# A hybrid trunk step: first transfers chained, x tiles loaded ahead, mLSTM outputs turned one step later, first attention tiles in other memory

## The chip, the cores and the metric

The kernel runs on one core of a Trainium2 chip, as one launch. The metric is the device time of that core in microseconds (us), from the first to the last instruction with what the launch adds around them. In the profile PE is TensorE (PEld its weight loads), DVE is VectorE, ACT is ScalarE, POOL is GpSimd and SP is SyncE, which here only issues transfers.

## The reference

One inference step of a one-layer trunk: 2048 prompt tokens (one sequence) and 64 sample tokens (8 sequences of 8 tokens, each with 8192 past positions in a paged cache). Two groups of heads share one input projection and one output projection: 8 heads of forgetting attention (FoX, width 64) and 4 heads of mLSTM (width 128). Everything is float32.

```
z = x @ w_in                       # x: 2048 or 64 tokens x 1024; w_in: 1024 x 3600
fq, fk, fv, f-gate = z[...]        # FoX queries, keys, values, log forget gates
mq, mk = silu(conv4(z[qk part]))   # causal convolution over 4 tokens, per channel
mv, i-gate, f-gate, o-gate = z[...]
fox = softmax(fq fk^T / 8 + L_q - L_k) fv      # L: running sum of the log forget gates
C, n, m, h = mLSTM scan over chunks of (mq, mk, mv, gates)
mix = [fox, layernorm_per_head(h) * norm_w * sigmoid(o-gate)] @ w_o
x1 = layernorm(alpha x + mix)
y  = layernorm(alpha x1 + relu(x1 @ w1)^2 @ w2)
```

The sample tokens run the same with keys, values and forget gates gathered from the paged cache through `page_table`, and with the mLSTM and convolution states that are given. Outputs are y, the new k and v, the log forget gates and the new states.

## The kernel before

**Phases.** Phase A (0 to about 965 us) makes the input projection for four blocks of four prompt tiles of 128 tokens (the first block also has tile 16, the 64 sample tokens), and beside it the mLSTM and the first part of the sample attention. Phase B is the prompt's FoX attention, phase O the output projection, phase C the MLP, with the rest of the sample attention beside it. A matmul of full precision is three matmuls of split operands: `mm3` (lines 154 to 156) multiplies the high parts (`whi`, `xh`) and the two mixed products (`wlo`, `xl`). `split_hi` (line 146, ACT) and `split_lo` (line 149, DVE) make these parts.

**Order.** The Python code names the work in a program order; a scheduler then orders the instructions on each engine by that and by their dependences. `tick(us)` is called after each piece of matmul work with its length. It advances two side programs written as generators: `macc` (the gate streams and the mLSTM, a step for each 2.3 us) and `acc` (the sample attention, a step for each 5.6 us in phase A). `acc[0]` is the time on its clock, `acc[1]` the generator, `attend` makes one step of it.

**x.** `load_x` (line 263) loads a tile of x into `xn` (two buffers), turns it with eight transposes (`px`, line 278, in the ring `pm` of four PSUM tiles that the projection uses too) and splits it to `xh` and `xl`. In `natural` (line 415, tokens on the output's partitions) a hook loads and turns tile n + 2 ahead of tile n's matmuls. The first two tiles of the next block are loaded and turned by the last `natural` of a block and after the block. `wload` (line 228) loads a weight block as two pieces of 512 KB (`wra`, line 236) and splits them. All these transfers are issued by SP, in its order.

**The convolution** of block 0 (`qi`, `qs`, `ac`, `scT`, lines 456 to 498) is mostly DVE's work. Beside it starts `sample_attention`: its prologue makes the gather indices (`idxK`, `idxV`, lines 1289 and 1295) and running sums of the forget gates (`ri`, line 1321) on DVE. After four such steps it waits until `kx["new"]` is set, late in the first block.

**The mLSTM** (`m_block`, line 617) runs in 16 chunks of 128 tokens: scores `pS` (line 642), transposed keys `pk` (line 655), numerators `mn` (lines 665, 666), state (line 674), then `norm_out` (line 569), whose last steps are a multiplication on POOL (`hh`, line 582). The result is turned by four transposes on PE (line 587), copied by ACT (`ot`, line 589) and stored; `turn_out` does this in the next chunk, right after its scores. `pS`, the turned output, `pk` and `mn` share a ring `mm` of two PSUM tiles:

```
            V.scalar_tensor_tensor(Wm, pS, KSC, Wm, op0=OP.mult, op1=OP.mult)
            yield 1
            turn_out()
            while bi not in gated:
                yield 1
            og = pm.tile([128, 512], F32, name="og", bufs=1)
            SY.dma_start(og, dog[t0:t0 + 128])
            yield 1
            pk = ppm.tile([128, 4, 128], F32, name="mm", tag="mm", bufs=2)
```

**Phase B** goes through 64 units of a head and 256 queries. For the first, `head` makes the tiles `nl`, `vn`, `ks`, `ls`, `keys` loads (`dup`), doubles and turns keys, `queries` loads and splits queries (`qn`, `qh`). The pool of these tiles takes memory that phase A's tiles had, so a first writer can have to wait for their last reader.

Of the kernel before, what the change touches and what calls it, by code (L numbers as in the profile page):

```python
# [10 lines left out]
F32 = mybir.dt.float32  # L11
# [13 lines left out]
D = 1024  # L25
# [17 lines left out]
C_V = 2568  # L43
# [9 lines left out]
def body(ctx, tc, I, O, stages):  # L53
# [142 lines left out]
    def conv_setup():  # L196
# [19 lines left out]
        SY.dma_start(gbias[:, 12:16], dap(I["b_fg"], 0, [[0, 128], [1, 4]]))  # L216

    hist = pa.tile([128, 8, 3], F32, name="hist")
    V.memset(hist, 0.0)
# [6 lines left out]
    mend = pa.tile([4, 1], F32, name="mend")  # L226

    def wload(cols):

        n = sum(c[1] for c in cols)  # L230
        H, L = [], []
        for kg in range(2):
            wr = pa.tile([128, 4 * 272], F32, name="wra", bufs=2)[:, :4 * n].rearrange("p (k c) -> p k c", k=4)
            o = 0
            for c0, m in cols:
                SY.dma_start(wr[:, :, o:o + m], w_in[kg * 512:(kg + 1) * 512, c0:c0 + m].rearrange("(k p) c -> p k c", p=128))
# [25 lines left out]

    def load_x(bi, tiles):

        blk, pre, off = geom(bi)
        for t in tiles:
            i = int(off[t] >= pre + 256)
            if len(xT.setdefault(bi, [])) == i:
                w = 256 if i else 320
                xT[bi].append((pa.tile([128, 8, w], F32R, name=f"xh{i}"), pa.tile([128, 8, w], F32R, name=f"xl{i}")))  # L270
            n = tok_n(t)
            xn = pa.tile([128, D], F32, name="xn", bufs=2)
            SY.dma_start(xn[:n], x_of(t))
            (xh, xl), s = xcol(bi, t)
            for hf in range(2):
                px = ppa.tile([128, 4, 128], F32, name="px", tag="pm", bufs=4)
                for k in range(4):
                    T.transpose(px[:, k, :n], xn[:n, (hf * 4 + k) * 128:(hf * 4 + k + 1) * 128], ident[:n, :n])
                dh = xh[:, hf * 4:hf * 4 + 4, s]
                split_hi(dh, px[:, :, :n])  # L280
                split_lo(xl[:, hf * 4:hf * 4 + 4, s], px[:, :, :n], dh)

# [128 lines left out]
    def block_a(bi):  # L411
        blk, pre, off = geom(bi)
        t0 = blk[-4] * 128
        c0 = blk[-4]
        def natural(sink, *cols, hook=None):
            wh, wl = first.pop() if first else wload(cols)
            for i, t in enumerate(blk):
                if hook:
                    hook(i)
                m = tok_n(t)  # L420
                ps = ppa.tile([128, 512], F32, name="pm", tag="pm", bufs=4)[:m, :wh[0].shape[1]]
                (xh, xl), s = xcol(bi, t)
                for k in range(8):
                    mm3(ps, xh[:, k, s], xl[:, k, s], wh[k], wl[k], k == 0, k == 7)
                sink(t, m, ps)
                tick(2.6)

        def stage(ps, m, n):
            st = pa.tile([128, 256], F32, name="st", bufs=4)[:m, :n]
            A.copy(st, ps)  # L430
            return st

        for i in range(2):
            def sink(t, m, ps, i=i):
                r = tok_r(t)
                SY.dma_start(dv[r:r + m, i * 256:(i + 1) * 256], stage(ps[:, :256], m, 256))
                if i == 1:
                    V.tensor_copy((gats if t == 16 else gat[:, t])[:, 0:16], ps[:, 256:272])
            natural(sink, (C_V + i * 256, 256), *([(C_FF, 8), (C_I, 8)] if i == 1 else []),
                    hook=None if i else lambda n: load_x(bi, blk[n + 2:n + 3]))  # L440
        if bi == 0:
# [113 lines left out]
        for i in range(2):  # L555
            def sink(t, m, ps, i=i):
                d = v_out(t)[:, i * 256:(i + 1) * 256]
                SY.dma_start(d, stage(ps, m, 256))
            natural(sink, (1024 + i * 256, 256),
                    hook=None if i == 0 or bi == 3 else lambda n: load_x(bi + 1, BLKS[bi + 1][0:1]) if n == len(blk) - 1 else None)  # L560

# [55 lines left out]
    def m_block(bi):  # L617
# [10 lines left out]
        for c in range(bi * 4, bi * 4 + 4):  # L628
# [17 lines left out]
            yield 1  # L646
            turn_out()
            while bi not in gated:
                yield 1
            og = pm.tile([128, 512], F32, name="og", bufs=1)  # L650
            SY.dma_start(og, dog[t0:t0 + 128])
            yield 1
            pk = ppm.tile([128, 4, 128], F32, name="mm", tag="mm", bufs=2)
            for h in range(4):
# [168 lines left out]
    if "S" in stages:  # L823
        gen = sample_attention(tc, I, O, ps_, pps, cst, ident, sqk, dnl, dR, dmix, dqb, vx, kx, pa)
    load_x(0, [16])
    first = [wload([(C_V, 256)])]
    load_x(0, [0])
    for bi in range(4):
        g = block_a(bi)
        next(g)  # L830
        if bi == 0 and gen:
            acc[0], acc[1] = 0.0, gen
        macc[1].append(m_block(bi))
# [5 lines left out]
        if bi < 3:  # L839
            load_x(bi + 1, BLKS[bi + 1][1:2])  # L840
    while macc[1]:
# [8 lines left out]
    def phase_b():  # L850
# [14 lines left out]

        def head(h):
            nl = pb.tile([128, 2048], F32, name="nl", bufs=2)
            vn = pb.tile([128, 16, 64], F32, name="vn", bufs=2)
            ks = pb.tile([128, 2048], F32R, name="ks", bufs=2)
            ls = pb.tile([128, 32], F32, name="ls", bufs=2)  # L870
            G.memset(ls, 1.0)
            return dict(h=h, ls=ls, nl=nl, vn=vn, ks=ks)
# [13 lines left out]

        def keys(z, g):

            h = z["h"]
            kn = twice(kp[g * 512:(g + 1) * 512, h * 64:h * 64 + 64], 4)  # L890
            if h == 0 and g == 0:
                queries(z, 0)
            if h == 0:
# [99 lines left out]
        def finish(z, half):  # L993
# [9 lines left out]
            for q in range(2):  # L1003
# [4 lines left out]
                SY.dma_start(dmix[h // 2, (h % 2) * 64:(h % 2) * 64 + 64, o + q * 512:o + q * 512 + 512], ot[:, s])  # L1008

        units = [(h, g) for h in range(8) for g in range(8)]  # L1010
        Z = {0: head(0)}
        dmask = pb.tile([128, 128], F32, name="dmask")
        V.memset(dmask, 0.0)
        G.affine_select(dmask, dmask, pattern=[[-1, 128]], compare_op=OP.is_ge, fill=NEG, base=0, channel_multiplier=1)
        keys(Z[0], 0)
# [33 lines left out]
    acc[1] = acc[3]  # L1049
    if acc[1] is not None:  # L1050
        attend()

# [210 lines left out]
def sample_attention(tc, I, O, ps_, pps, cst, ident, sqk, dnl, dR, dmix, dqb, vx, kx, pa):  # L1263
# [309 lines left out]
    def step(n):  # L1573
# [84 lines left out]
```

## Time and profile before

| | |
|---|---|
| time, median of 3 runs | 3442.84 us (3429.21 to 3446.31) |
| the profiled execution | 3431.24 us, span 3429.5 us |
| mean granted TensorE clock | 0.983 |
| busy: PE, DVE, ACT, POOL | 96%, 63%, 40%, 26% |
| moved by DMA | 646.37 MB, mean 188 GB/s |

Rows of a timeline read: start, length, engine, line, operation, out<-in, shape, number of instructions drawn together, and in brackets the idle time of the engine ahead of it and what ended that. Rows of groups read: line, engine, operation, out<-in, shapes, number | busy us, mean ns | idle time before. Rows of windows: from:to, length, busy time of PE, PEld, DVE, ACT, POOL (with the number of instructions), granted clock (1.00 is full speed), share of the DMA engines, GB/s.

### The profile page before, as it was taken

The page shows a single profiled execution, that of the slowest core. Times are in us where ns is not written, and L with a number is a line of the kernel's source. Part 1 is how long each engine was busy: PE and PEld are TensorE (multiplying, and loading weights), DVE is VectorE, ACT ScalarE, POOL GpSimd, SP SyncE. Part 2 cuts the span into 40 slices and gives each one's busy share as a digit, 9 for nine tenths or more (in the row PEclk, how much of TensorE's full clock was granted, in tenths as well). Part 3 has the DMA queues.
Part 4 walks back from the last instruction along what each step waited for, and adds up shares of the span by engine and source line. Part 5 has one row for each costly group of instructions (what it writes and reads, how often), then busy time and mean ns, then how long its engine had stood idle before and what let it go on. Part 6 is the DMA issues. An engine that isn't in the chain of part 4 may idle for free.

```text
span 3429.5 us, 59557 instructions
## 1 busy us (share of the span) xinstructions
PE 3277.8 (96%) x22428; PEld 2675.2 (78%) x22428; DVE 2166.7 (63%) x5282; ACT 1367.5 (40%) x2818; POOL 892.0 (26%) x958
## 2 busy tenths in 40 slices
PE   8999989988979999999899999999999999999998
PEld 8999988888866666677577777777777777888887
DVE  5847657557558787655566666666666545655545
ACT  3332334333348888512323233332333333443332
POOL 0021222322332222276323324323324210100000
PEclk9999999999989999999899999999999999999999
DMA  5565764876753232487777777768668554442221
GB/s 170 133 204 160 226 203 141 293 227 202 237 178 89 75 82 58 139 284 250 257 248 255 246 236 260 273 227 301 231 209 305 199 185 151 154 139 81 82 85 65
DMA packets 427095, 646.37 MB, mean 188 GB/s; under 512 B 84092, under 2 KB 320960, under 8 KB 425912
## 3 DMA queue, kind: packets, MB, share of 16 engines
q1 hardware_dynamic: 350120, 363.35, 35.0%
q0 software_dynamic: 74304, 270.57, 21.5%
q10 hardware_dynamic: 2384, 8.65, 0.7%
q8 instruction: 177, 2.90, 0.3%
q14 instruction: 110, 0.90, 0.1%
HBM read 589.63 MB, written 52.83 MB: 187 GB/s over the span
## 4 chain that ended last, share of the span: by engine, by line
PE 43%; DMA 4%; issue 2%; DVE 1%; POOL 0%; ACT 0%; POOLq 0%; ACTq 0%; SPq 0%; DVEq 0%
PE py L154 7%; PE py L155 7%; PE py L156 7%; PE ph L154 6%; PE ph L155 6%; PE ph L156 6%; PE sO L1541 2%; PE sQ L1429 2%; DMA kT<-cache_k,idxK 1%; DMA wr<-w 1%; DMA vt<-cache_v,idxV 1%; PE sT L1498 1%; DVE wl L149 0%; DMA y_prompt<-y 0%; PE px L1168 0%
## 5 line engine op out<-in xcount | busy, mean ns | idle before, releaser
L1225 DVE TENSOR_TENSOR y<-y,py 128x512 f32<-128x512 f32 (+1 forms) x476 | 320.5, 679 | 293.2 <-PE py L156 289.1
L1406 DVE STREAM_TRANSPOSE kT<-kT 128x512 f32<-128x512 f32 x512 | 330.3, 685 | 215.5 <-DMA kT<-cache_k,idxK 215.3
L154 PE MATMUL ph<-x1h,wh 128*128 128x512 f32 (+1 forms) x1280 | 454.1, 355 | 3.8 <-ACT wh L146 2.3
L156 PE MATMUL ph<-x1h,wl 128*128 128x512 f32 (+1 forms) x1280 | 451.2, 354 | 4.3 <-DVE wl L149 4.3
L155 PE MATMUL ph<-x1l,wh 128*128 128x512 f32 (+1 forms) x1280 | 453.1, 354 | 0.0
L1400 POOL DMA_INDIRECT kT<-cache_k,idxK x256 | 264.3, 1032 | 702.6 <-PE sQ L1429 637.8
L154 PE MATMUL py<-wh,hh 128*128 128x512 f32 (+1 forms) x1088 | 432.2, 399 | 3.4 <-DVE y L1223 2.4
L146 ACT ACTIVATE wh<-wr 128x1024 fp32r<-128x1024 f32 x264 | 273.0, 1056 | 400.9 <-PE py L156 194.9
L155 PE MATMUL py<-wl,hh 128*128 128x512 f32 (+1 forms) x1088 | 427.6, 393 | 0.0
L156 PE MATMUL py<-wh,hl 128*128 128x512 f32 (+1 forms) x1088 | 427.0, 393 | 0.0
L149 DVE TENSOR_TENSOR wl<-wr,wh 128x1024 fp32r<-128x1024 f32 x264 | 329.5, 1252 | 78.7 <-PE ph L156 24.4
L154 PE MATMUL pm<-whi,xh 128*128 128x256 f32 (+2 forms) x1088 | 321.4, 295 | 14.1 <-ACT ch_n L506 5.6
L155 PE MATMUL pm<-wlo,xh 128*128 128x256 f32 (+2 forms) x1088 | 314.2, 289 | 0.0
L156 PE MATMUL pm<-whi,xl 128*128 128x256 f32 (+2 forms) x1088 | 313.9, 289 | 0.0
L154 PEld LDWEIGHTS ph<-x1h,wh 128*128 128x128 f32 x1280 | 241.3, 188 | 43.3 <-issue 4.9
L156 PEld LDWEIGHTS ph<-x1h,wl 128*128 128x128 f32 x1280 | 240.8, 188 | 39.3 <-DVE wl L149 6.2
L155 PEld LDWEIGHTS ph<-x1l,wh 128*128 128x128 f32 x1280 | 241.1, 188 | 36.2 <-issue 2.9
L154 PEld LDWEIGHTS py<-wh,hh 128*128 128x128 f32 (+1 forms) x1088 | 201.4, 185 | 61.9 <-issue 11.9
L156 PEld LDWEIGHTS py<-wh,hl 128*128 128x128 f32 (+1 forms) x1088 | 201.3, 185 | 49.6 <-issue 2.5
L155 PEld LDWEIGHTS py<-wl,hh 128*128 128x128 f32 (+1 forms) x1088 | 201.6, 185 | 41.2 <-issue 2.5
L154 PE MATMUL pm<-xh,whi 128*128 128x256 f32 (+1 forms) x768 | 225.2, 293 | 5.8 <-ACT qi L469 5.8
L1517 POOL DMA_INDIRECT vt<-cache_v,idxV x158 | 162.6, 1029 | 257.1 <-PE sO L1541 187.2
(365 smaller groups left out, 6886.0 us busy)
## 6 DMA issues: line engine op xcount, KB each, us to landing
wr<-w SPq DMA_DIRECT2D x256, 512.0 KB
wra<-w_in SPq DMA_DIRECT2D x112, 512.0 KB
xn<-x_prompt SPq DMA_DIRECT2D x32, 512.0 KB
Rb<-dR SPq DMA_DIRECT2D x128, 128.0 KB
qn<-dq SPq DMA_DIRECT2D x128, 64.0 KB
wr<-w_o SPq DMA_DIRECT2D x16, 512.0 KB
xr<-dmix SPq DMA_DIRECT2D x16, 512.0 KB
dx<-xn SPq DMA_DIRECT2D x16, 512.0 KB
```

The costliest lines, as they stand in the source:

```text
L146: last["ACT"] = A.activation(dst, src, AF.Copy, scale=scale)
L149: r = (eng or V).tensor_tensor(dst, src, hi.bitcast(F32), op=OP.subtract)
L154: T.matmul(ps, wh, xh, start=first, stop=False)
L155: T.matmul(ps, wh, xl, start=False, stop=False)
L156: last["PE"] = T.matmul(ps, wl, xh, start=False, stop=stop)
L1225: V.tensor_tensor(y, y, ps, op=OP.add)
L1400: G.indirect_dma_start(out=piece(n), out_offset=None, in_=ck, in_offset=IO(ap=idxK[:, b, j // 2, j % 2:j % 2 + 1], axis=0))
L1406: V.transpose(x, x)
L1429: r = T.matmul(pq[h4 * 32:h4 * 32 + 32, hg].rearrange("p (k f c) -> p k f c", k=2, f=4), z["qb"][:, hd], kv, start=(db == 0), stop=(db == ...
L1498: T.transpose(p[:, f], z["U"][u][:, hg, f].rearrange("p k t -> p (k t)"), ident)
L1517: G.indirect_dma_start(out=vt.rearrange("p f c -> p (f c)"), out_offset=None, in_=cv, in_offset=IO(ap=idxV[:, b, (kt % 4) * 4 + kt // 4, f ...
L1541: after_ = T.matmul(po[r:r + 32], z["PT"][:, hg, 2 * f + g, pg].rearrange("p h q -> p (h q)"), vts[f][:, g, hg * 256:(hg + 1) * 256], star ...
```

## The change

- `load_x` is split into `x_load` (the transfer) and `x_turn` (transposes and splits), and the transfers are named earlier: at the start tiles 16 and 0, the first weights, then 1 and 2 between the turns; for later blocks the first two tiles at the first tile of the last `natural`, the third and fourth behind the first two turns. In the first block tile n + 2 is turned after tile n's matmuls, not ahead of them.
- `first` ties the first eight of these transfers (x tiles and weight pieces) in the order of the program.
- `turn_out` comes one `yield` later, after the load of `og` and right ahead of `pk`.
- `acc[0]` starts at -12 and not at 0 when the sample attention begins.
- In phase B the first keys and queries are loaded ahead of `head`, and the tiles are allotted in another order. The two `qs` tiles are touched once at the start.
- In the sample attention of phase C the V gathers of a step stand ahead of its K gathers; the step that takes the sample attention up again behind phase B is made in phase B's units 10 to 15, one gather for each.

```
+    for _ in range(2):
+        V.memset(pa.tile([128, 8, 11], F32, name="qs", bufs=2)[:, 0, 0:1], 0.0)
...
+    head = [0, None]
+    def first(r):
+        if head[0] < 8:
+            if head[1] is not None:
+                tc.add_manual_dep(r.ins, head[1].name,
+                                  mybir.DependencyInfo(mybir.DependencyClass.NoSync, mybir.DependencyReason.DATA), reason="first")
+            head[0] += 1
+            head[1] = r.ins
...
-                SY.dma_start(wr[:, :, o:o + m], w_in[...])
+                first(SY.dma_start(wr[:, :, o:o + m], w_in[...]))
...
+    def x_load(*tiles):
+        for t in tiles:
+            xns[t] = pa.tile([128, D], F32, name="xn", bufs=2)
+            first(SY.dma_start(xns[t][:tok_n(t)], x_of(t)))
+    def x_turn(bi, t):                 # the rest of load_x
...
+        def turn_next(n):
+            for t in blk[n + 2:n + 3]:
+                x_turn(bi, t)
+                if bi == 0:
+                    x_load(*blk[n + 4:n + 5])
-                    hook=None if i else lambda n: load_x(bi, blk[n + 2:n + 3]))
+                    **({} if i else {"hook" if bi else "after": turn_next}))
...
-            natural(sink, (1024 + i * 256, 256),
-                    hook=None if i == 0 or bi == 3 else lambda n: load_x(bi + 1, BLKS[bi + 1][0:1]) if n == len(blk) - 1 else None)
+            def turn_first(n):
+                if n == 0:
+                    x_load(*BLKS[bi + 1][0:2])
+                if n == len(blk) - 1:
+                    x_turn(bi + 1, BLKS[bi + 1][0])
+                    x_load(BLKS[bi + 1][2])
+            natural(sink, (1024 + i * 256, 256), hook=None if i == 0 or bi == 3 else turn_first)
...
             yield 1
-            turn_out()
             while bi not in gated:
                 yield 1
             og = pm.tile([128, 512], F32, name="og", bufs=1)
             SY.dma_start(og, dog[t0:t0 + 128])
             yield 1
+            turn_out()
             pk = ppm.tile([128, 4, 128], F32, name="mm", tag="mm", bufs=2)
...
-    load_x(0, [16])
-    first = [wload([(C_V, 256)])]
-    load_x(0, [0])
+    x_load(16, 0)
+    W0 = [wload([(C_V, 256)])]
+    x_turn(0, 16)
+    x_load(1)
+    x_turn(0, 0)
+    x_load(2)
...
-            acc[0], acc[1] = 0.0, gen
+            acc[0], acc[1] = -12.0, gen
...
-            load_x(bi + 1, BLKS[bi + 1][1:2])
+            x_turn(bi + 1, BLKS[bi + 1][1])
+            x_load(BLKS[bi + 1][3])
...
         def head(h):
+            vn = pb.tile([128, 16, 64], F32, name="vn", bufs=2)
             nl = pb.tile([128, 2048], F32, name="nl", bufs=2)
-            vn = pb.tile([128, 16, 64], F32, name="vn", bufs=2)
+            if h == 0:
+                masks.append(pb.tile([128, 128], F32, name="dmask"))
+            ls = pb.tile([128, 32], F32, name="ls", bufs=2)
             ks = pb.tile([128, 2048], F32R, name="ks", bufs=2)
-            ls = pb.tile([128, 32], F32, name="ls", bufs=2)
...
+        Z = {0: dict(h=0)}
+        kn = keys_load(0, 0)
+        queries(Z[0], 0)
+        Z[0].update(head(0))
...
+            if 10 <= n < 16 and acc[1] is not None:
+                attend()
...
     acc[1] = acc[3]
-    if acc[1] is not None:
-        attend()
...
+        if n >= 35 and (n % 2 == 1 or not vx["live"]):
+            while v_room():
+                v_gather()
         g, r = divmod(n - 2, 4)
...
-        if n >= 35 and (n % 2 == 1 or not vx["live"]):
-            while v_room():
-                v_gather()
...
             for i in range(6):
                 k_gather(NA + i)
+                if i < 5:
+                    yield 1
```

More of the change, by code (lines that the diff above doesn't have):

```diff
@@ L235, in wload @@
             for c0, m in cols:
-                SY.dma_start(wr[:, :, o:o + m], w_in[kg * 512:(kg + 1) * 512, c0:c0 + m].rearrange("(k p) c -> p k c", p=128))
+                first(SY.dma_start(wr[:, :, o:o + m], w_in[kg * 512:(kg + 1) * 512, c0:c0 + m].rearrange("(k p) c -> p k c", p=128)))
                 o += m
@@ L261, in geom @@
         return blk, pre, off
-    def load_x(bi, tiles):
-        blk, pre, off = geom(bi)
[L266 to L281, printed above, removed]
+    xns = {}
+    def x_load(*tiles):
[3 more added lines that the diff above has]
+    def x_turn(bi, t):
+        blk, pre, off = geom(bi)
+        i = int(off[t] >= pre + 256)
+        if len(xT.setdefault(bi, [])) == i:
+            w = 256 if i else 320
+            xT[bi].append((pa.tile([128, 8, w], F32R, name=f"xh{i}"), pa.tile([128, 8, w], F32R, name=f"xl{i}")))
+        n = tok_n(t)
+        xn = xns.pop(t)
+        (xh, xl), s = xcol(bi, t)
+        for hf in range(2):
+            px = ppa.tile([128, 4, 128], F32, name="px", tag="pm", bufs=4)
+            for k in range(4):
+                T.transpose(px[:, k, :n], xn[:n, (hf * 4 + k) * 128:(hf * 4 + k + 1) * 128], ident[:n, :n])
+            dh = xh[:, hf * 4:hf * 4 + 4, s]
+            split_hi(dh, px[:, :, :n])
+            split_lo(xl[:, hf * 4:hf * 4 + 4, s], px[:, :, :n], dh)
     def xcol(bi, t):
@@ L414, in block_a, with natural @@
         c0 = blk[-4]
-        def natural(sink, *cols, hook=None):
-            wh, wl = first.pop() if first else wload(cols)
+        def natural(sink, *cols, hook=None, after=None):
+            wh, wl = W0.pop() if W0 else wload(cols)
             for i, t in enumerate(blk):
@@ L425, in natural @@
                 sink(t, m, ps)
+                if after:
+                    after(i)
                 tick(2.6)
@@ L885, in forget_values, with keys_load, keys @@
             SY.dma_start(z["vn"][:, a // 128:(a + n) // 128], vp[a:a + n, h * 64:h * 64 + 64].rearrange("(t p) c -> p t c", p=128))
-        def keys(z, g):
+        def keys_load(h, g):
+            return twice(kp[g * 512:(g + 1) * 512, h * 64:h * 64 + 64], 4)
+        def keys(z, g, kn=None):
             h = z["h"]
-            kn = twice(kp[g * 512:(g + 1) * 512, h * 64:h * 64 + 64], 4)
-            if h == 0 and g == 0:
-                queries(z, 0)
+            kn = keys_load(h, g) if kn is None else kn
             if h == 0:
@@ L1008, in finish @@
                 SY.dma_start(dmix[h // 2, (h % 2) * 64:(h % 2) * 64 + 64, o + q * 512:o + q * 512 + 512], ot[:, s])
+        masks = []
         units = [(h, g) for h in range(8) for g in range(8)]
-        Z = {0: head(0)}
-        dmask = pb.tile([128, 128], F32, name="dmask")
+        Z = {0: dict(h=0)}
+        kn = keys_load(0, 0)
+        queries(Z[0], 0)
+        Z[0].update(head(0))
+        dmask = masks[0]
         V.memset(dmask, 0.0)
         G.affine_select(dmask, dmask, pattern=[[-1, 128]], compare_op=OP.is_ge, fill=NEG, base=0, channel_multiplier=1)
-        keys(Z[0], 0)
+        keys(Z[0], 0, kn)
         sc = {}
```

## The prediction

> **What bounds the kernel now.** I read the head of the page first, then the list of waits on TensorE (waited-for work, total us, times, longest).
>
> ```profile
> span 3429.5 us, 59557 instructions
> PE 3277.8 (96%) x22428; PEld 2675.2 (78%) x22428; DVE 2166.7 (63%) x5282; ACT 1367.5 (40%) x2818; POOL 892.0 (26%) x958
> ```
> ```profile
> PE px L278 <- DMA xn<-x_prompt: 16.9, 6, 5.6
> ...
> PE mm L587 <- POOL hh L582: 7.9, 4, 2.9
> PE pS L933 <- ACT qh L146: 7.8, 2, 5.9
> ...
> PE pm L154 <- DVE st L514: 3.7, 1, 3.7
> ...
> PE px L497 <- DVE scT L489: 2.4, 1, 2.4
> ```
>
> TensorE (PE) is busy 3277.8 of 3429.5 us, so all idle time together is 151.7 us, 4.4%. The edit adds no matmul and removes none; it can only win idle time back, and the half-speed clock that follows some idle stretches. The listed waits that it aims at are those above: 16.9 + 7.9 + 7.8 + 3.7 + 2.4 = 38.7 us, about 1.1%. The question is how many of them it reaches. The profiled execution took 3431.24 us (span 3429.5 plus 1.74 around it), 11.6 under the median of the three runs, 3442.84. I work out the change on the profiled execution and carry the difference over to the median. About 0.5%, 17.2 us, is what a measurement of this kernel can tell from no change; the three runs alone lie 17.1 apart.
>
> I also compared the order in which each engine's instructions stand in the two programs. From some 40 us after the start of phase B to the end (about 1010 to 3429 us) it is the same on all five engines. So the V gathers put ahead of the K gathers, and the sample attention's restart that was moved to units 10 to 15 of phase B, change nothing that an engine executes there: cost 0, and no cover is needed.
>
> **The start (chained transfers, x loaded ahead).** PE's rows, then SP's issues, then the first two weight casts on ACT and a split on DVE:
>
> ```profile
> 4.58 1.08 PE L278 MATMUL px<-ident,xn 64*128 64x64 f32 x8 [4.58 <-DMA xn<-x_sample]
> 8.69 1.97 PE L278 MATMUL px<-ident,xn 128*128 128x128 f32 x8 [3.04 <-DMA xn<-x_prompt]
> 11.55 1.94 PE L278 MATMUL px<-ident,xn 128*128 128x128 f32 x8 [0.89 <-DMA xn<-x_prompt]
> 13.15 0.56 PE L154 MATMUL pm<-whi,xh 128*64 128x256 f32 x1
> ...
> 19.85 1.06 PE L278 MATMUL px<-ident,xn 128*128 128x128 f32 x8 [3.04 <-DMA xn<-x_prompt]
> 20.67 0.36 PE L154 MATMUL pm<-whi,xh 128*128 128x256 f32 x1
> ```
> ```profile
> 23.74 0.93 PE L278 MATMUL px<-ident,xn 128*128 128x128 f32 x7
> 24.42 0.36 PE L154 MATMUL pm<-whi,xh 128*128 128x256 f32 x1
> ```
> ```profile
> 1.44 1.11 SPq L236 DMA_DIRECT2D wra<-w_in  x2
> 2.59 0.51 SPq L273 DMA_DIRECT2D xn<-x_prompt  x1
> ...
> 14.56 0.93 SPq L273 DMA_DIRECT2D xn<-x_prompt  x1
> ```
> ```profile
> 5.98 1.05 ACT L146 ACTIVATE whi<-wra 128x1024 fp32r<-128x1024 f32 x1
> 7.36 1.06 ACT L146 ACTIVATE whi<-wra 128x1024 fp32r<-128x1024 f32 x1 [0.34 <-DMA wra<-w_in]
> ```
> ```profile
> 7.06 1.22 DVE L149 TENSOR_TENSOR wlo<-wra,whi 128x1024 fp32r<-128x1024 f32 x1 [0.52 <-ACT whi L146]
> ```
>
> SP's order was x_sample, two weight pieces, x tile 0; it becomes x_sample, x tile 0, two weight pieces. By the rows the pieces arrive in the order of issue, some 1.4 us each: about 5.9, 7.3, 8.69. So tile 0's transposes run at 5.9 in place of 8.69, and the second weight piece is late by one place (8.69 in place of 7.36). PE's order becomes: sample transposes, tile 0 transposes, the sample's 24 matmuls, tile 1 transposes, tile 0's matmuls, tile 2 transposes, and so on. The sample's matmuls need the first piece cast (arrival 7.3, behind one cast of tile 0 on ACT, 0.60: start about 7.6, end 8.65) and its low half (1.22 on DVE: 9.9). They start at about 9.9 in place of 13.15. At half clock first, as before, they end at 14.3. Tile 2's load was issued at 14.56 behind five weight transfers, and that made the 3.04 us wait at 19.85; now it stands on SP's queue behind small transfers only, waits for tile 0's transposes to free its buffer (7.9), and is there long before its use at about 18.3. The wait goes. Counting on: tile 1 transposes to 15.4, tile 0's 24 matmuls (20.67 to 23.74 before, less a few slow ones and a transpose: 2.9, so 0.12 each) to 18.3, tile 2 transposes to 19.3; tile 1's matmuls start there, in place of 24.42. Tile 3's transposes, already done by 24.42 before, are still to come, 0.8 us. **Gain 24.42 - 19.3 - 0.8 = 4.3; I take 4** (bounds 2, if ACT casts the late second piece another 2 us later, to 5). What is queued behind SP's new waits: the second weight block, issued some 5 us later than before. It is used at the end of the first block's tiles, near 29 us, 10 us after it lands, so it costs 0; were that cover gone it would cost those 5.
>
> The same loading ahead for blocks 1 to 3 changes nothing: a tile's load has only two buffers, stands at the same place of SP's order, and still waits for the same transposes. These waits stay, the longest of them here:
>
> ```profile
> 727.34 1.94 PE L278 MATMUL px<-ident,xn 128*128 128x128 f32 x8 [5.61 <-DMA xn<-x_prompt]
> ```
>
> **The sample attention's prologue, 12 us of pace later.** Windows (length, busy of PE, PEld, DVE, ACT, POOL, clock, DMA), PE's waits inside them, and what DVE does there:
>
> ```profile
> 96.00:107.00 11.00, 9.09 (x70) 8.53 (x68) 10.75 (x47) 4.07 (x10) 0.82 (x1) 1.00 0.58 103
> 107.00:117.00 10.00, 4.74 (x26) 4.25 (x27) 9.79 (x22) 2.71 (x10) 2.22 (x3) 0.82 0.49 150
> 117.00:133.00 16.00, 16.00 (x124) 15.99 (x123) 13.49 (x37) 6.21 (x14) 0.00 (x0) 0.90 0.32 81
> ```
> ```profile
> 105.31 0.83 PE L497 MATMUL px<-ident,scT 128*24 128x128 f32 x6 [1.05 <-ACT qi L469]
> 108.58 0.28 PE L497 MATMUL px<-ident,scT 128*24 128x128 f32 x1 [2.44 <-DVE scT L489]
> ...
> 116.75 0.48 PE L154 MATMUL pm<-whi,xh 128*128 128x256 f32 x1 [3.68 <-DVE st L514]
> ...
> 133.00 0.83 PE L642 MATMUL mm<-qk 128*128 128x128 f32 x6
> ```
> ```profile
> L1295 DVE TENSOR_SCALAR idxV<-ptf,fo 32x128 int32<-32x128 f32 x8 | 3.4, 448 | 0.1
> ...
> L1321 DVE TENSOR_TENSOR_SCAN ri<-onesr,lg 128x128 f32<-128x128 f32 x8 | 2.7, 398 | 0.0
> ...
> L1289 DVE TENSOR_SCALAR idxK<-ptf,fo 32x128 int32<-32x128 f32 x8 | 2.0, 277 | 0.1
> ```
>
> From 96 to 117 DVE is busy 20.5 of 21 us and PE waits 1.05 + 2.44 + 3.68 = 7.2. In the new order the prologue (3.4 + 2.7 + 2.0, with its small operations about 10 us) stands behind two more steps of the convolution. The first two waits go. In exchange PE comes to the last conv state (scT) after 22 matmuls in place of 48; adding up DVE's rows it is ready at about 110.4 and PE is there at 107.9: a new wait of 2.5. The old wait for st then lies three tiles later and is covered. But DVE's total is the same, and at the end of this stretch PE needs the last qk product (first used at 133.00). DVE can't deliver that earlier than its 34 us of work less the 2.5 us that it idles in the last window: 130 to 132. By then PE has 22 matmuls (2.6 us) more behind it than in the old order. **Gain 2.6 + about 1.5 = 4** (bounds 0, if DVE's backlog eats all of it, and 6.5, the waits less what little stays). Any half clock after the new gap is inside this, because the end is set by DVE.
>
> **mLSTM outputs turned one step later.** PE's rows for three of the four waits, the multiply on POOL that ends the second, the clock behind that, and the copy on ACT that follows the third:
>
> ```profile
> 440.92 0.94 PE L587 MATMUL mm<-ident,hh 128*128 128x128 f32 x4 [2.52 <-POOL hh L582]
> ```
> ```profile
> 468.96 1.12 PE L587 MATMUL mm<-ident,hh 128*128 128x128 f32 x4 [2.86 <-POOL hh L582]
> ```
> ```profile
> 892.26 0.66 PE L587 MATMUL mm<-ident,hh 128*128 128x128 f32 x4 [1.84 <-POOL hh L582]
> ```
> ```profile
> 465.59 3.32 POOL L582 TENSOR_TENSOR hh<-hh,og 128x512 f32<-128x512 f32 x1 [3.35 <-DMA va<-dv]
> ```
> ```profile
> 469.50:473.00 3.50, 3.50 (x23) 3.50 (x22) 0.40 (x2) 0.96 (x2) 0.00 (x0) 0.66 0.80 191
> ```
> ```profile
> 894.67 0.58 ACT L589 COPY ot<-mm 128x512 f32<-128x512 f32 x1
> ```
>
> At 468.96 the transposes move behind 8 more matmuls and POOL's multiply ahead of four gathers; at 892.26 behind 26 matmuls (3.1 us). Both waits go: 2.86 + 1.84 = 4.7. At 440.92 the turn moves by one row only (it and the next transposes stood together already): its 2.52 stays. The fourth, 7.9 - 2.52 - 2.86 - 1.84 = 0.7, sits at the end of phase A and stays. The clock after the second wait was 0.66 over 3.5 us: 1.2 us more. **Gain 5.9** (bounds 3, if the next wait takes half, and 8.5 with 440.92 too). What is late next: the copy on ACT, now nearer to its reader.
>
> On the clock: the row says a gap of 2.86 us was followed by 3.5 us at 0.66. [...]
>
> **Phase B's first tiles in other memory.** SP issues the same transfers in the same order; only waits on memory reuse differ. The largest wait there,
>
> ```profile
> 976.24 1.12 PE L933 MATMUL pS<-ks,qh 128*128 128x384 f32 x2 [5.91 <-ACT qh L146]
> ```
>
> hangs on the second half of the queries, issued behind phase A's last output, which is not moved. I take 0.3 (0 to 1; below 0 nothing speaks, as no transfer is added). Two added memsets on DVE at the start lie in its idle time: 0.
>
> **Sum:** 4 + 4 + 5.9 + 0.3 = 14.2 us, bounds 5 and 21. Profiled execution 3431.24 - 14.2 = 3417.0; on the median 3442.84 - 14.2 = 3428.6, and I write **3428**.
>
> **Rivals.** *All named waits go.* If the loads ahead also remove the boundary waits and phase B starts at once, the whole 38.7 us go (the 1.05 at 105.31 and the 1.2 of clock with them: 41), which gives about 3402. For it: each wait is named in the profile. Against: neither the x loads of later blocks nor the second half of the queries stand earlier on SP. Chance 0.15, with its milder forms (one of the two).
>
> *DVE or DMA give it back.* The first 130 us are DVE's, and the block boundaries wait for transfers; if what PE gains ahead is waited for at the first of these, only the turn's 5.9 or less remains: 3437 to 3443, within 0.5%. The row at 727.34 speaks for it, a transfer queue that can be the clock of a boundary; the DMA share of 0.3 to 0.6 in the windows above speaks against. Chance 0.20.
>
> *Slower: the turn runs into the ring of two PSUM tiles.* The turned output, the turned keys and the numerators share two buffers. With the turn one step later, the first numerator follows it after about one tile (24 x 0.12 = 2.9 us) and needs the copy on ACT finished. At 892.26 that copy ended 894.67 + 0.58 - 892.26 = 3.0 us after the turn began. At 16 chunks it takes over (14.2 + 17.2) / 16 = 2.0 us of extra wait per chunk to come out slower by more than 0.5%, so the copy must end 4.9 us after the turn; with 2.9 us per chunk, as long a wait as the longest one there is now, the time is 3442.84 - 14.2 + 46 = 3475. Against it: at 440.92 the two already stand together without such a wait. Chance 0.10.
>
> *The change does nothing on the chip* (the arrival of x tile 0 does not follow the order of issue, PE finds other waits): 3443, chance 0.10. [...]
>
> **Numbers.** The forecast itself has 0.45. Its own time is spread by the runs' +-8 around 3428, so that a third of it lies beyond 17.2 us: faster 0.15 + 0.21 = 0.36 and a little of the others, 0.38; slower 0.10 and the runs' spread on the do-nothing case, 0.12; within 0.5% the remaining 0.50. The range reaches down to the first rival with its 3402 and up to the do-nothing case with the runs' spread, 3403 to 3450; the slow rival is left out.
>
> **What would show it.** Right: the first unbroken matmul stretch starts near 19 to 20 us with no 3.04 wait; no waits at 105 and 108, one of 2 to 3 us for scT near 106 (all times 4 us earlier); no turn wait near 455 and 880, one of 2.5 us near 430; the boundary wait of 5.6 unchanged. Wrong: numerators waiting for the copy ot; a turn wait elsewhere; weights of the second block late near 25 us; a stretch after 1010 us whose length differs by more than 2 us.

## The result and the profile after

The changed kernel took 3428.94 us (median of 10 runs, 3425.28 to 3435.19), the kernel before on the same chip 3440.82 us (10 runs, 3429.21 to 3446.61). The ratio is 0.9969 with a 95% interval of 0.9956 to 0.9982: some 11 us less (6 to 15), and within the 0.5% that the prediction called no change. The forecast was 3428 and a gain of 14.2, from 3442.84; the kernel before stands 2.0 lower in these runs.

The profiled execution of the changed kernel took 3425.96 us. First the page's head, then the waits on PE that answer to those shown of before.

```profile
span 3424.3 us, 59559 instructions
PE 3283.5 (96%) x22428; PEld 2680.0 (78%) x22428; DVE 2167.4 (63%) x5284; ACT 1366.2 (40%) x2818; POOL 886.2 (26%) x958
```
```profile
PE px L296 <- DMA xn<-x_prompt: 7.6, 3, 5.4
PE mm L687 <- DVE Wm L677: 6.7, 3, 5.2
PE pS L972 <- ACT qh L146: 6.6, 2, 4.7
...
PE pm L154 <- ACT cs_n L524: 3.5, 1, 3.5
...
PE mm L619 <- POOL hh L614: 2.7, 2, 2.0
```

Lines have moved: 278 is now 296, 587 is 619, 655 is 687, 645 is 677. The waits for x fell from 16.9 to 7.6, those of the turn for POOL from 7.9 to 2.7. Those for st (3.7) and scT (2.4) are gone, and cs_n stands in their place with 3.5. One line is new, and the prediction did not have it: the turned keys wait 6.7 us for Wm on DVE.

**Where the time came from.** The projection's matmuls run in the same order in all these kernels, so the time at which one of them starts can be compared. At four places of the profile, in us:

| kernel | behind the start (39 us) | behind the convolution (158) | at 498 us | near the end of phase A (931) | end of the span |
|---|---|---|---|---|---|
| before, first profile | 39.1 | 157.9 | 497.6 | 930.6 | 3429.5 |
| before, second profile | 40.1 | 158.1 | 499.5 | 931.7 | 3431.4 |
| changed, first | 34.8 | 148.4 | 484.9 | 924.3 | 3424.3 |
| changed, second | 35.9 | 149.5 | 488.1 | 926.2 | 3419.7 |

So, in these profiles, the changed kernel is 4.3 ahead after the start, 9 to 10 past the convolution, 11 to 13 at 498, and only 5.5 to 6.3 at 931. It makes its gain in the first 500 us, and hands half of it back in the next 430 (the profiles of set three, below, show it otherwise). From about 1081 us on, the traces have each engine's instructions in the same order before and after, and single executions scatter: from 931 us to the end 2498.9 and 2499.7 us before, 2500.0 and 2493.4 changed. The time of the runs is therefore read from their medians, and the profiles up to 931.

The start (PE; the fourth and fifth rows are transposes of tiles 1 and 2, the last but one the first matmul of tile 1, the last the first with the second weight block):

```profile
4.39 3.11 PE L296 MATMUL px<-ident,xn 64*128 64x64 f32 x16 [4.39 <-DMA xn<-x_sample]
8.28 0.48 PE L154 MATMUL pm<-whi,xh 128*64 128x256 f32 x1 [0.78 <-ACT whi L146]
9.54 0.48 PE L155 MATMUL pm<-wlo,xh 128*64 128x256 f32 x1 [0.78 <-DVE wlo L149]
13.69 1.03 PE L296 MATMUL px<-ident,xn 128*128 128x128 f32 x8
17.43 1.04 PE L296 MATMUL px<-ident,xn 128*128 128x128 f32 x8
```
```profile
18.23 0.36 PE L154 MATMUL pm<-whi,xh 128*128 128x256 f32 x1
...
30.25 0.47 PE L154 MATMUL pm<-whi,xh 128*64 128x272 f32 x2 [0.80 <-ACT whi L146]
```
```profile
29.08 1.11 ACT L146 ACTIVATE whi<-wra 128x1088 fp32r<-128x1088 f32 x1 [3.59 <-DMA wra<-w_in]
```

Tile 0's transposes follow the sample's without a gap, the sample's matmuls run on from 9.54, and the two waits of 3.04 are gone. One wait is new: ACT casts the second half of the second weight block only at 29.08 (19.96 before), and PE waits 0.80 for that. The convolution, in windows and by PE's two waits there:

```profile
101.00:111.00 10.00, 6.84 (x45) 6.82 (x46) 9.66 (x35) 4.21 (x13) 2.44 (x4) 0.83 0.55 173
111.00:127.00 16.00, 15.67 (x133) 15.47 (x131) 15.69 (x44) 5.55 (x11) 0.00 (x0) 1.00 0.28 81
```
```profile
104.16 0.33 PE L154 MATMUL pm<-whi,xh 128*64 128x256 f32 x1 [3.47 <-ACT cs_n L524]
```
```profile
126.68 0.49 PE L674 MATMUL mm<-qk 128*128 128x128 f32 x2 [0.33 <-DVE qk L508]
```

One wait of 3.47 is left of three that were 7.2 together, and 0.33 for the last qk product; DVE (third number) is as full as before, 25.4 of 26 us.

**Where it went.** The new wait, on PE, on DVE and on POOL:

```profile
902.45 1.06 PE L674 MATMUL mm<-qk 128*128 128x128 f32 x8
...
909.10 0.60 PE L619 MATMUL mm<-ident,hh 128*128 128x128 f32 x4
914.88 1.12 PE L687 MATMUL mm<-ident,qk 128*128 128x128 f32 x4 [5.18 <-DVE Wm L677]
```
```profile
910.62 1.30 DVE L1450 STREAM_TRANSPOSE kT<-kT 128x512 f32<-128x512 f32 x2 [8.08 <-DMA kT<-cache_k,idxK]
911.85 1.18 DVE L149 TENSOR_TENSOR wlo<-wra,whi 128x1024 fp32r<-128x1024 f32 x1
912.95 1.29 DVE L1450 STREAM_TRANSPOSE kT<-kT 128x512 f32<-128x512 f32 x2
914.17 0.65 DVE L677 SCALAR_TENSOR_TENSOR Wm<-mm,Wm 128x512 f32<-128x512 f32 x1
```
```profile
902.04 1.27 POOL L614 TENSOR_TENSOR hh<-hh,og 128x512 f32<-128x512 f32 x1
903.49 1.06 POOL L1444 DMA_INDIRECT kT<-cache_k,idxK  x1 [0.17 <-issue]
904.86 0.94 POOL L1444 DMA_INDIRECT kT<-cache_k,idxK  x1 [0.30 <-issue]
```

POOL issues the K gathers behind its multiplication of hh, when PE has begun the chunk's scores (902.45). DVE has their transposes ahead of Wm in its order, and waits 8.08 us for the first gather, issued at 903.49 and used at 910.62. Wm stands behind them, and the turned keys need the PSUM tile that Wm reads. In the kernel before Wm stands behind such transposes as well, and DVE idles 6.72 us for their gather. But there POOL issues it ahead of the multiplication and 12.6 us ahead of the chunk's scores (916.80). DVE's wait is over before the scores begin, and the turned keys (923.86) wait for nothing:

```profile
904.23 0.94 POOL L1400 DMA_INDIRECT kT<-cache_k,idxK  x1 [4.38 <-PE sQ L1429]
...
916.75 2.15 POOL L582 TENSOR_TENSOR hh<-hh,og 128x512 f32<-128x512 f32 x1 [2.39 <-issue]
```
```profile
911.72 1.30 DVE L1406 STREAM_TRANSPOSE kT<-kT 128x512 f32<-128x512 f32 x2 [6.72 <-DMA kT<-cache_k,idxK]
...
922.32 0.65 DVE L645 SCALAR_TENSOR_TENSOR Wm<-mm,Wm 128x512 f32<-128x512 f32 x1
```
```profile
916.80 1.05 PE L642 MATMUL mm<-qk 128*128 128x128 f32 x8
...
923.86 0.60 PE L655 MATMUL mm<-ident,qk 128*128 128x128 f32 x4
```

What the wait costs here is more than itself, for the clock falls behind it (windows of 3.5 us):

```profile
914.90:918.40 3.50, 3.50 (x17) 3.50 (x18) 3.13 (x7) 0.00 (x0) 0.00 (x0) 0.50 1.03 385
918.40:921.90 3.50, 3.50 (x23) 3.50 (x23) 1.58 (x3) 1.45 (x3) 0.00 (x0) 0.69 0.74 242
```

5.2 + 3.5 x 0.50 + 3.5 x 0.31 = 8.0 us, and the lead falls from 14.3 to 6.3 between the matmuls that the kernel before starts at 915 and at 931.

### The profile page after: what moved, and what is told of

It reads as the page before. It is cut to its first block, busy times and chain, and to the rows that moved or that the text cites. A ratio compares the mean times of both kernels' runs of the same rounds, so it can differ in the third digit from the quotient of the medians.

```text
span 3424.3 us, 59559 instructions
## 1 busy us (share of the span) xinstructions
PE 3283.5 (96%) x22428; PEld 2680.0 (78%) x22428; DVE 2167.4 (63%) x5284; ACT 1366.2 (40%) x2818; POOL 886.2 (26%) x958
## 4 chain that ended last, share of the span: by engine, by line
PE 42%; DMA 4%; issue 2%; DVE 2%; ACT 1%; POOL 0%; SPq 0%; ACTq 0%; POOLq 0%; DVEq 0%
PE py L154 7%; PE py L155 6%; PE py L156 6%; PE ph L154 6%; PE ph L155 6%; PE ph L156 6%; PE sO L1585 2%; DMA wr<-w 2%; PE sQ L1473 2%; DMA kT<-cache_k,idxK 1%; DMA vt<-cache_v,idxV 1%; DVE wl L149 1%; PE sT L1542 0%; ACT wh L146 0%; DMA xr<-cache_v,idxV 0%
## 5 line engine op out<-in xcount | busy, mean ns | idle before, releaser
L156 PE MATMUL pm<-whi,xl 128*128 128x256 f32 (+3 forms) x1088 | 313.8, 289 | 0.0
```

What stands on the lines that cost most here:

```text
L156: last["PE"] = T.matmul(ps, wl, xh, start=False, stop=stop)
```

## The experiments

The experiments ran in three sets, each on a chip of its own; the times of before beside them were 3436.80 (set one: one to four), 3438.38 (set two: five, six and the second profiles) and 3457.42 (set three: seven, eight and the changed kernel a third time). Ratios are to the kernel before of the same set. Single profiles are read for stands and waits, the runs for time.

The question after the result: which part does what, and whose is the new wait. My theory: the gain is the start's and the prologue's; -12 is two paces of 5.6 and a remainder of 0.8, and the remainder shifts the sample attention's later steps against the mLSTM, which takes away the wait at 467 and makes the one at 910. The rival is the prediction's step: the turn takes away the one, and by the ring of two PSUM tiles makes the other.

**One: the start alone.**

```
         (the changed kernel with)
-            turn_out()   behind the load of og
+            turn_out()   where it was
-            acc[0], acc[1] = -12.0, gen
+            acc[0], acc[1] = 0.0, gen
         (and phase B as before)
```

> Only the start and the loads of x are changed: chained transfers, x loaded ahead; turn, pace of the sample attention and phase B are as before. Theory (the parts add up): the first stretch of matmuls is 4.3 us ahead of the kernel before from 39 us on and stays so to the end of phase A, with the waits of 2.4 and 3.7 us at 106 and 113 us still there (at about 102 and 109); time 4 us under the kernel before. Rival (the gain is given back, since DVE is full from 60 us on): the 4.3 us are gone by 120 us, and the time is that of before.

Ratio 0.9987 (0.9972 to 1.0003), 3430.97 us. In the profile the lead is 4.3 at 39 and at 95 us, 5.3 at 158, 6.9 at 498. The waits of 2.45 and 3.98 are there, at 101 and 107. So DVE does not eat the start's gain, and this rival falls. But at 931 the kernel is 2.4 us behind the kernel before: between 498 and 931 it lost 9, without the wait for Wm. The time points to some 4 us less, and the interval includes none.

**Two: the sample attention's clock alone.**

```
-            acc[0], acc[1] = 0.0, gen
+            acc[0], acc[1] = -12.0, gen
```

> Only the sample attention's clock is changed: it starts at -12. Theory (12 is two paces of 5.6 and a remainder of 0.8; the two paces move the prologue, the remainder shifts every later step against the mLSTM): 5 us ahead at 140 us; at about 467 us the wait for POOL's multiplication is gone (POOL makes it ahead of four K gathers), some 4 us more; and near 920 us a new wait of 4 to 6 us for DVE, which has K transposes ahead of the scores' product Wm and waits for their gathers, 8 us with the slow clock behind it. In all about 0 to -3 us. Rival (the turn one step later makes the wait near 920 us and takes away the one at 467 us): neither is seen here, the wait of 2.9 us at 467 stays, and the time is 5 us under before.

Ratio 0.9964 (0.9945 to 0.9983), 3428.23 us. Relative to its own stand at 95 us it is 5.1 us ahead at 158. No wait for POOL stands at 467, and the new wait is here without the turn:

```profile
926.21 0.66 PE L655 MATMUL mm<-ident,qk 128*128 128x128 f32 x4 [3.26 <-DVE Wm L645]
```

with 5.2 us for Wm between 860 and 930 in all. The mechanism came as expected, the time did not: 12 us less (6 to 19; the medians lie 8.6 apart) in place of 0 to 3. The profiled execution, 3430.77 us, shows only some of that, and behind this wait the matmuls came 0.12 us apart (927.26 to 927.97), as ahead of it (920.04 to 922.67).

**Three: the turn alone.**

```
             yield 1
-            turn_out()
             while bi not in gated:
                 yield 1
             og = ...
             yield 1
+            turn_out()
             pk = ...
```

> Only the turn of the mLSTM's outputs stands one step later. Theory: the wait of 1.8 us at 890 goes, of the 2.9 us at 467 some 1 us goes (8 matmuls stand ahead of the turn now, POOL still has its gathers ahead of the multiplication), and no new wait for Wm comes near 920 us; 2 to 4 us under before. Rival (the ring of two PSUM tiles): the wait for Wm of over 4 us near 920 us is here, and the time is that of before or over it.

Ratio 1.0001 (0.9985 to 1.0017), 3436.30 us. Of the wait of 1.84 at 890, 0.68 is left (at 896), that at 467 is still 2.65, and Wm makes 1.2 us at most. Neither the gain that the theory left to the turn (2 to 4 us) nor the rival's loss can be seen in the time.

```profile
469.93 0.66 PE L587 MATMUL mm<-ident,hh 128*128 128x128 f32 x4 [2.65 <-POOL hh L582]
```

**Four: two paces exactly.**

```
         (the changed kernel with)
-            acc[0], acc[1] = -12.0, gen
+            acc[0], acc[1] = -11.2, gen
```

> The changed kernel with the sample attention's clock at -11.2, two paces exactly, and not -12. Theory (the remainder of 0.8 makes the wait near 910 us): the prologue still moves (10 us ahead at 140 us), the wait of 5.2 us for Wm near 910 us is gone and the 8 us with its slow clock, part of the wait for POOL near 457 us comes back (1 to 2 us); 4 to 6 us under the changed kernel, some 16 to 18 under before. Rival (the turn makes it): the wait near 910 us stays, and the time is that of the changed kernel or 2 us over it.

Ratio 0.9962 (0.9943 to 0.9981), 3424.69 us. The wait for Wm is gone. The one near 457 is back in full, and so is the one near 890, though the turn is one step later:

```profile
460.71 0.66 PE L619 MATMUL mm<-ident,hh 128*128 128x128 f32 x4 [2.85 <-POOL hh L614]
...
890.72 0.66 PE L619 MATMUL mm<-ident,hh 128*128 128x128 f32 x4 [1.88 <-POOL hh L614]
```

On DVE, K transposes that wait 3.01 and 1.66 us for their gathers stand ahead of the hh that POOL's multiplication needs at 457 (456.19 here); in the changed kernel that hh comes at 445.58, ahead of them. So all three waits follow the remainder of 0.8, and not the turn. The 4 to 6 us that I expected on top of the changed kernel can't be seen. The times of the two overlap (13 and 11 us under before, each by 4 to 7 either way), and the stretch from 498 to 931 took 439.7, as long as in the changed kernel, with 11.2 us of waits for V gathers in it in place of 4.8:

```profile
PE sO L1585 <- DMA vt<-cache_v,idxV: 11.2, 5, 3.8
```

**Second profiles of both kernels.** No edit.

> The kernel before, unchanged, profiled a second time. Theory (its first trace had a fast stretch from 498 to 931 us: the same stretch took 435 to 442 us in four of the five other kernels, and 433 us in this one): 436 to 440 us here, with the rest of the span within 3 us of the first trace, and a time of 3434 to 3440 us. Rival (that stretch is a property of the kernel before): 432 to 434 us again.

432.2 us, time 3433.08: the rival holds for this kernel. The first trace was not a lucky one: both profiles of the kernel before have this stretch shorter (432 to 433) than any other kernel of sets one and two (434.7 to 442.3).

> The changed kernel, unchanged, profiled a second time. Theory (the wait for Wm near 910 us follows from the order of the gathers on POOL and the transposes on DVE): a wait of the turned keys for Wm is there again between 880 and 915 us, 2 to 6 us in all; the first stretch is 4.3 us ahead and 140 us some 9 to 10 us ahead of the kernel before, as in its first trace. Rival (chance of one execution): no such wait.

Time 3421.36. The wait is there again: 6.3 us for Wm, the longest 4.1, at 914. The first stands are those of the first trace plus about 1 us; half of it is x_sample's later arrival (4.93 in place of 4.39).

**Five: five paces.**

```
-            acc[0], acc[1] = -12.0, gen
+            acc[0], acc[1] = -28.0, gen
```

> The changed kernel with the sample attention's clock at -28, five paces exactly. Theory (DVE is full from 60 to 133 us, and the prologue of 10 us is what is too much): with the prologue behind the convolution the wait of 2.8 to 3.5 us near 101 us gets under 1 us, and the matmuls are 12 to 14 us ahead of the kernel before at 140 us, 3 to 4 more than with two paces; the rest is as with two paces; time 2 to 5 us under that of two paces. Rival (DVE's own convolution is the limit there): the wait near 101 us keeps over 2 us and the stand at 140 us is the same 10 us.

Ratio 0.9971 (0.9957 to 0.9985), 3425.02 us. The rival holds. The prologue's first operations are at 123.7 now, behind all of the convolution, and PE's wait at 101 is longer still:

```profile
105.29 0.28 PE L523 MATMUL px<-ident,scT 128*24 128x128 f32 x1 [4.25 <-DVE scT L515]
```

The stand at 158 is 10.3 us ahead, 6.3 of them gained since 95 us, where two paces gave 5.2. The one wait left there is for scT, whose copy stands in DVE's order while DVE is full (11.00 of 11 us from 96 to 107). That this is the convolution's own work is read from the trace, not tried.

**Six: the changed kernel without the turn.**

```
         (turn_out() back where it was)
```

> The changed kernel with the turn of the mLSTM's outputs put back where it was. Theory (the turn is worth one wait of 1.8 us): the wait near 457 us stays away, since POOL's order comes from the clock of the sample attention and not from the turn; the wait for Wm near 910 us stays; time within 3 us of the changed kernel. Rival (the prediction's step, the turn brings 5.9 us): 4 to 8 us over the changed kernel, with a wait of some 2.9 us for POOL at 457.

Ratio 0.9971 (0.9953 to 0.9989), 3424.65 us. No wait near 457, none for the turn near 880, a wait for Wm of 3.55 at 913 (the matmuls behind it came 0.12 us apart from 914.19 to 914.90, as ahead of it), and no loss against the changed kernel that the runs can tell. Both waits that the prediction's 5.9 us were made of stay away without the turn, so the term falls.

**Seven: phase B and what follows alone.**

```
         (the kernel before with head, keys_load, queries, dmask,
          V gathers ahead of K gathers and attend in units 10 to 15 of the changed one)
```

> Only the parts of phase B and of the sample attention behind it are changed (first tiles in other memory, first keys and queries ahead, V gathers ahead of K gathers, restart in units 10 to 15); phase A is as before. Theory (the order of instructions on all five engines is that of the kernel before, only waits on memory differ): the waits at the start of phase B stay at 2 to 3 us for ks and 4 to 6 us for qh, the time is that of before within 0.15%. Rival (the new places in memory start phase B at once): the wait for qh gets under 2 us, and the time 5 us under before.

Ratio 1.0002 (0.9991 to 1.0014). The waits at the start of phase B are 5.1 for qh and 2.8 for ks. This part does nothing that can be measured, as predicted (0.3).

**Eight: start and five paces, no turn; and the changed kernel a third time.**

> The changed kernel with the turn put back and the sample attention's clock at -28: the start's part, five paces and no remainder. Theory (start and prologue carry the gain, the turn nothing; what is gained by 500 us is given back in part by 930 us): 10 to 14 us under before, within 4 us of the changed kernel; no wait for Wm over 2 us near 910 us; some 9 to 11 us ahead at 158 us and at least 3 us given back between 498 and 931 us. Rival (the gain of each part is kept to the end): 14 us or more under before, and over 5 us under the changed kernel, whose wait for Wm is gone here.

> The changed kernel, unchanged, beside the two others on the same chip. 9 to 13 us under before; the stretch that the kernel before makes from 498 to 931 us takes 437 to 441 us, with a wait for Wm of 3 to 6 us in it.

0.9973 (0.9962 to 0.9983) and 0.9966 (0.9954 to 0.9978), in us 3448.93 and 3445.76 beside 3457.42. The time is 8.5 under before (5.9 to 13.1 by the interval), a little short of the theory's 10 to 14, and 3.2 over the changed kernel, within its 4. At 158 us it is 9.9 ahead of seven, which has phase A as before, and Wm makes 1.8 at most in one wait. But the give-back is not as expected. In this set the stretch from 498 to 931 took 446.4 us with phase A as before (seven), 445.3 in eight and 441.2 in the changed kernel. So nothing is given back there in this set, and the changed kernel even gains, its wait for Wm (4.2) included. No version that I made beats the changed kernel by more than its interval.

## Why the prediction was right, and where it was not

The time was right to 1 us, and that is luck: the sum was right by terms that were not. The start and the prologue brought about what was booked. The two waits booked to the turn (4.7 us) did go, but not by the turn, and a wait that nobody had booked took more than that in the first profile.

- **The start, 4 predicted (4.3 counted): 4.3, by two errors that cancel.** The counted 9.9, 14.3, 15.4, 18.3 and 19.3 were 9.5 (the first matmul that ran on), 13.7, 14.5, 17.4 and 18.2 on the chip: tile 1's first matmul came at 18.23, which is worth 24.42 - 18.23 - 0.8 = 5.4. But the second weight block, booked at 0 under a cover of 10 us, was late. SP issued its pieces from 11.91 to 17.43, some 2 us later than before (9.42 to 15.54), yet ACT cast the second half 9 us later, with the DMA engines at 1.02 to 1.07 from 16 to 28 us. PE idles 0.80 at 30.25, the sign that the prediction named for being wrong there. Past it the lead is 4.3. It is not lost to the full DVE (experiment one).
- **The prologue, 4 predicted: 5.1 to 5.3** between 95 and 158 us against the first profile of the kernel before, in the changed kernel, in two and in four (the changed kernel's second profile against that of the kernel before: 4.4). The reason held: DVE's total sets the end of the stretch, where PE waits 0.33 us for the last qk product. Of the 5.2 us in the changed kernel 3.4 are waits, the rest matmuls at a higher clock (0.97 in place of 0.95). The new wait was 3.47 in place of 2.5, and it was for cs_n, the copy on ACT behind the same conv state, not for scT itself. Experiment five shows the limit from the other side: with all of the prologue gone from there PE still waits 4.25.
- **The turn, 5.9 predicted: about 0.** This is the step that failed, and it failed by its cause. The order of POOL (multiplication ahead of four gathers) that takes away the 2.86 at 467 was booked as the turn's, and so was the end of the 1.84 at 890. Both come from the remainder of 0.8 us in -12. In the eight profiles with the clock at 0, -11.2 or -28 the sixth turn waits 2.6 to 4.0 us and the thirteenth 0.7 to 3.4, with the turn moved (three, four, five) or not. In the five with -12 neither waits at all, moved or not (two and six). The turn alone took at most a part of the wait at 890, and the time shows no gain from it. The prediction named every queue at this place but read the new order as the work of one edit, when two of them could have moved it.
- **A wait that the prediction did not have.** The same remainder puts a K gather behind the multiplication at 902, and with it DVE's transposes and Wm: 5.2 us and 2.8 of clock in the first profile. It is there in all five profiles with -12: 5.2, 4.1 and 4.2 us in the changed kernel, 3.3 in two and 3.6 in six (behind these two the matmuls came 0.12 us apart, behind the first profile's 0.21), and at most 1.2 us in that chunk in the eight others. In the eight, POOL issues the first K gather 10 to 16 us ahead of the chunk's scores, in the five within about 1 us of them. No other remainder was tried. The slow rival was near: PE waits on the ring of two PSUM tiles in the chunk's turned keys. But what is late is Wm behind a gather on DVE, not the copy on ACT, and the turn is not its reason.
- **The clock.** The 1.2 us booked behind the gap of 2.86 could not be counted on. Windows of 3.5 us behind a gap of 2.52 (before), of 1.98 and of 2.21 (the same gap in the first and second profile of the changed kernel) and of 2.85 (four):

```profile
440.90:444.40 3.50, 3.48 (x17) 3.48 (x18) 1.64 (x5) 0.78 (x2) 0.00 (x0) 0.54 0.69 144
```
```profile
433.90:437.40 3.50, 3.50 (x32) 3.50 (x31) 2.26 (x5) 0.72 (x2) 0.00 (x0) 1.00 0.77 135
```
```profile
433.90:437.40 3.50, 3.50 (x19) 3.50 (x19) 2.26 (x5) 0.58 (x1) 0.00 (x0) 0.53 0.72 176
```
```profile
460.70:464.20 3.50, 3.49 (x30) 3.49 (x31) 1.13 (x4) 0.59 (x1) 0.00 (x0) 1.00 0.86 203
```

  The clock was 0.54, 1.00, 0.53 and 1.00: the longest of these gaps cost no clock, and one place of one kernel did and did not. So in these profiles the length of a gap does not tell whether the clock falls behind it, and what decides it is not shown.
- **Blocks 1 to 3, phase B, everything after: 0 to 0.3 predicted, none measured.** The boundary wait of 5.6 is 5.4, the ratio of experiment seven is 1.0002. The order of the instructions was read wrong by 70 us: in the traces it is the same only from about 1081 us on, not from 1010.
- **The rival "given back", 0.20.** Half of it is true. Not DVE at 120 us, but the stretch from 498 to 931 gave back 6 to 7 us of the changed kernel's lead in its first two profiles. The wait for Wm accounts for as much; but one and four lose 9 and 7 without it, and in set three nothing is lost.

**What stays open.** Why the stretch from 498 to 931 is shortest with the kernel before's phase A in the first profiles and longest in set three. The windows say where the difference lies (kernel before, one, seven; behind the length stands PE's busy time):

```profile
497.60:930.60 433.00, 398.14 (x3640) 369.14 (x3639) 278.50 (x723) 153.87 (x335) 132.62 (x143) 0.98 0.70 226
```
```profile
490.70:933.00 442.30, 403.84 (x3640) 373.42 (x3640) 279.62 (x723) 152.81 (x335) 135.49 (x143) 0.97 0.68 221
```
```profile
498.90:945.30 446.40, 409.92 (x3640) 376.76 (x3640) 280.17 (x723) 152.46 (x335) 132.72 (x143) 0.96 0.68 219
```

PE makes the same matmuls. It idles 34.9, 38.5 and 36.5 us, and is busy for 398, 404 and 410 us at a granted clock of 0.98, 0.97 and 0.96. So 5.7 of the 9.3 us that one loses here, and 11.8 of the 13.4 that seven takes longer, are matmuls at a lower clock and not waits. In four it is 5.2 of 6.7, in the changed kernel 3.4 of 6.4. The same goes for the whole span of set three: of the 32.7 us between the profiled executions of seven and of the kernel before, 22.0 are PE's busy time (3299.8 and 3277.8). Why the clock was lower more of the time is not shown. The pace alone gains 12 us in time and shows 0.5 to 2.3 against the two profiled executions of the kernel before: with executions of one kernel up to 23 us apart in one set (3428.49 to 3451.47) I can't say where the rest is.

## What to carry to other kernels

Where a scheduler orders the engines, compare the order with each edit undone before an effect is booked to one of them: here a phase shift of 0.8 us, and not the edit that was made for it, decided which of two waits a chunk had. Ask of every gain far from the end what the next work that runs on its own time will make of it: here 14 us of lead became 6 in one profile. And read an engine's wait for when the work behind it is needed: with the same Wm behind both, 6.7 us of idle DVE ahead of the scores cost nothing, and 8.1 us of it behind them cost PE 8.

## What the hardware showed that I had not expected

The granted clock fell to 0.53 over 3.5 us behind a gap of only 2.21 us, while behind one of 3.55 the matmuls kept the 0.12 us apart that they had ahead of it (six, 914.19 to 914.90). The kernel before took 3437 to 3441 us in three sets of runs and 3457 in the last, with ratios between kernels that held (0.9969, 0.9966). The three sets of experiments ran on three chips; whether it is the chip is not shown. A K gather issued at 903.49 was there for DVE only at 910.62, 7 us later, with the DMA engines at 0.72 over that stretch.
